# Products of old states with C placed behind weights' low parts, and logs of decays loaded one group at a time

## The chip, the cores and the metric

The kernel runs on one core of one Trainium2 chip, in one launch. The core has TensorE (PE in the profile; PEld is its loading of weights), VectorE (DVE), ScalarE (ACT) and GpSimd (POOL), which compute, and SyncE (SP), whose queue issues most of the transfers. The metric is the time of one execution on the device in microseconds, as the median over runs.

## The reference

One step of a hybrid decoder layer, for a prompt of 256 rows and 8 sequences that each decode one row. All of it is fp32; the model width is 2048. One input projection feeds windowed attention and a state-space mixer (32 heads of 64 in 4 groups, 128 states each); their outputs go through one output projection. Cross-attention and a convolutional feed-forward part follow, which the change doesn't touch.

```python
def ssd_scan(xs, dt, a, bm, cm, h0, chunk):
    ...
    la = jnp.cumsum(dt * a, axis=2)
    xdt = xs * dt[..., None]
    seg = la[:, :, :, None] - la[:, :, None, :]
    decay = jnp.exp(jnp.where(causal, seg, -jnp.inf))
    cb = jnp.einsum('bclgn,bcsgn->bclsg', cm, bm)
    y = jnp.einsum('bclsgh,bcsghp->bclghp', cb[..., None] * decay, xdt)
    decay_end = jnp.exp(la[:, :, -1:] - la)
    states = jnp.einsum('bcsgn,bcsghp->bcghpn', bm, xdt * decay_end[..., None])
    ...
    y = y + jnp.einsum('bclgn,bcghpn->bclghp', cm, h_prev) * jnp.exp(la)[..., None]

def ssd_mixer(z, xbc, dt_raw, conv_past, h0, ...):
    xbc, conv_new = causal_dwconv(xbc, conv_past, conv_w, conv_b)
    xbc = jax.nn.silu(xbc)
    ...
    y, h_last = ssd_scan(...)
    y = y + xs * d_skip
    y = y.reshape(b, t, D_SSD) * jax.nn.silu(z)
    y = rms_norm(y, norm_g)

def _layer(x, ...):
    proj = rms_norm(x, g_mix) @ w_in
    q, k, v, z, xbc, dt_raw = jnp.split(proj, IN_SPLITS, axis=-1)
    attn = swa_banded(q, k, v, sinks)        # or swa_step for the decode rows
    ssd, new_conv, new_h = ssd_mixer(z, xbc, dt_raw, ...)
    x = x + jnp.concatenate([attn, ssd], axis=-1) @ w_out
    x = x + cross_attend(x, ...)
    f, new_ffn = conv_ffn(x, ...)
    return x + f, ...
```

For a decode row the scan is one step: the output is C times the old state (128 states by 64 by 32 heads, for each sequence), scaled with the decay, plus what the row itself brings. These products of the old state with C are the 32 products of the title: a tile of 128 x 512 each, for one of 16 blocks of channels and four of the eight sequences.

## The kernel before

*Weights.* Every projection streams its weights from memory through weights() in parts of 128 x 1024 (512 KB, tile wraw, four buffers, issued on SP, L83). ScalarE rounds a part to its high half whi (L89), VectorE subtracts to get the low half wlo (L90), four buffers of each. mm3() multiplies in three passes, high by high, high by low, low by high (L104, L105, L106), so a part gives 24 matmuls with 264 columns (256 prompt rows and 8 decode rows). Parts 0 to 95 are w_in, 96 to 111 the first half of w_out, which meets the attention's output AT; from 112 on w_out meets the mixer's output Y.

*Order.* The code is not in the order in which it runs. A scheduler gives every instruction a place on its engine by the order of the code and by priority: weights() stands at high priority, and "with tc.issue_after(x)" puts what is inside behind x. Each engine then works through its list strictly in order, so an instruction that waits holds up all that is behind it. Tiles come from pools with few buffers: a load into a tile can't be issued before the last reader of that buffer is done.

*The mixer.* conv_group(g), g = 0 to 3, projects four blocks of channels of x by two calls of conv_pair (four weight parts each), does the causal convolution and SiLU for them (L769 on ScalarE, L771 and L773 on VectorE) and the decode rows by conv_sample. z_pair(i), i = 0 to 7, projects two blocks of the gate z and multiplies it into y. ssd_prompt(g) is the scan of the prompt for one group in two chunks. logs() loads what it needs: the cumulated logs of the decays, broadcast over partitions, into one tile called late (two loads of 512 KB, L824, and two of 128 KB, L828, on SP). Then ScalarE takes Relu of differences of logs (L846, 16 of 128 x 128 per group) and Exp (L847 twice, L889), VectorE multiplies with the products of C and B (L848), TensorE forms the output (L876) and the state of each chunk (L866), ScalarE copies the state of the first chunk to hp (L869), and the second chunk takes it up (L887, L894, L895).

*The decode rows' old states.* ssd_sample(g) loads C of the eight sequences, broadcast over partitions, into cb (512 KB, one buffer, on POOL's queue, L911); then, eight times, a piece of the old state into h (256 KB, three buffers, POOL's queue, L916), the product with cb (L917) and the sum over the states (L918), both on VectorE. The results ych are used only in gate_sample(), which finishes the decode rows of Y; it stands behind w_out's unit 4. It is called four times, behind conv_group(0), z_pair(1), z_pair(5) and w_out's unit 0. The scheduler is free to spread a call's instructions.

Of the kernel before, what the change touches and what calls it, by code (L numbers as in the profile page):

```python
# [7 lines left out]
F32 = mybir.dt.float32  # L8
F32R = mybir.dt.float32r
AF = mybir.ActivationFunctionType  # L10
ALU = mybir.AluOpType
# [37 lines left out]
def hybrid_decoder_step_kernel(ctx: ExitStack, tc: tile.TileContext, I, O):  # L49
    nc = tc.nc  # L50
# [25 lines left out]
    def weights(src, n=2048, into=None):  # L76

        out = []
        with tc.high_priority():
            for o in range(0, n, NPART):  # L80
                w = min(NPART, n - o)
                x = raw_part(w)
                marks["load"] = nc.sync.dma_start(out=x, in_=src[:, o:o + w])  # L83
                if into:
                    hi, lo = into
                else:
                    hi = wpool.tile([128, w], F32R, tag="whi", name="whi", bufs=WBUFS)
                    lo = wpool.tile([128, w], F32R, tag="wlo", name="wlo", bufs=WBUFS)
                S.copy(out=hi, in_=x)  # L89
                V.tensor_tensor(out=lo, in0=x, in1=hi.bitcast(F32), op=ALU.subtract)  # L90
                out.append((hi, lo))
        return out

# [5 lines left out]
                V.scalar_tensor_tensor(out=lo, in0=x, scalar=g, in1=hi.bitcast(F32), op0=ALU.mult, op1=ALU.subtract))  # L99

    marks = {}

    def mm3(out, wh, wl, xh, xl, start, stop):
        PE.matmul(out, wh, xh, start=start, stop=False)  # L104
# [94 lines left out]
    with tc.manual_schedule(engines={mybir.EngineType.SP, mybir.EngineType.PE, mybir.EngineType.Activation, mybir.EngineType.DVE}):  # L199
# [21 lines left out]
        for k in range(6):  # L221
            x_hi(k)
            lo = w_split(k, 1, k < 2)
# [74 lines left out]
    def total(acc, n, name, w=T, pool=None):  # L298
        p = psum("y")
        PE.matmul(p[:, :w], ones, acc, start=True, stop=True)  # L300
        r = pool.tile([128, w], F32, name=name) if pool else small.tile([128, w], F32, tag="r", name=name, bufs=2)
        rms(r, p[:, :w], n)
        return r
# [221 lines left out]
    def attn_prompt(j, rq, nrq, c, tag):  # L525
# [30 lines left out]
        for h in range(2):  # L556
            for kb in range(nb):
                tr(p[:, (h * nb + kb) * 128:(h * nb + kb) * 128 + 128], e[:, h, kb * 128:kb * 128 + 128])
        pt = mp.tile([128, 4, 128], F32, tag=tag, name="pt", bufs=2 if tag == "bc" else 1)
        S.copy(out=pt[:, 0:2 * nb, :], in_=p[:, 0:2 * nk].rearrange("p (a q) -> p a q", q=128))  # L560
        return pt

# [223 lines left out]
    def conv_pair(b0, dst):  # L786
        us = next_u()
        in_pair(lambda m, pm: V.tensor_tensor(out=us[:, m, 3:], in0=pm, in1=r0, op=ALU.mult))
        conv_side(b0, us, dst)
# [29 lines left out]
    def logs():  # L819

        g = len(lates)
        w = apool.tile([128, 8 * PITCH], F32, tag="B", name="late", bufs=4)
        for c in range(2):
            nc.sync.dma_start(out=w[:, 1024 * c:1024 * c + 1024].rearrange("p (h l) -> p h l", h=8),  # L824
                              in_=dram_la[c, 8 * g:8 * g + 8, :].partition_broadcast(128))
        ti = w[:, 2048:2560].rearrange("p (i l) -> p i l", i=4)
        for h in range(2):
            nc.sync.dma_start(out=ti[h * 64:h * 64 + 64], in_=lav[h][4 * g:4 * g + 4, :].partition_broadcast(64))  # L828
        lates.append(w)
# [76 lines left out]

    ych = mp.tile([128, KB, 8], F32, name="ych")

    def ssd_sample(g):
        cb = mp.tile([128, 8, 128], F32, tag="cb", name="cb", bufs=1)  # L910
        nc.gpsimd.dma_start(out=cb, in_=dram_bc[1][8 * g:8 * g + 8, :].partition_broadcast(128))  # L911
        for q in range(2):
            rows = slice(4 * q, 4 * q + 4)
            for i in range(4):
                h0 = mp.tile([128, 4, 128], F32, tag="h0", name="h0", bufs=3)
                nc.gpsimd.dma_start(out=h0, in_=I["h0"][4 * g + i][:, rows, :])  # L916
                V.tensor_tensor(out=h0, in0=h0, in1=cb[:, rows, :], op=ALU.mult)  # L917
                V.tensor_reduce(out=ych[:, 4 * g + i, rows], in_=h0, op=ALU.add, axis=AX.X)  # L918

    def conv_group(g):  # L920
        for i in (0, 2):
            conv_pair(4 * g + i, xs[g][:, i:i + 2, :TP])
        gs = slice(4 * g, 4 * g + 4)
        x = ysam[:, gs, :]
        conv_sample(4 * g, x)
        V.tensor_tensor(out=xds[:, gs, :], in0=x, in1=dsb[:, gs, 0:8], op=ALU.mult)
        V.tensor_tensor(out=x, in0=x, in1=pc("d_skip", 4 * g, 4).unsqueeze(2).broadcast_to([128, 4, 8]), op=ALU.mult)
# [43 lines left out]
        res.append(r)  # L971

    conv_group(0)
    ssd_sample(0)
    logs()
    logs()
    conv_group(1)
    ssd_prompt(0)
    conv_group(2)
    with tc.issue_after(marks["load"].ins):  # L980
# [3 lines left out]
    with tc.issue_after(marks["load"].ins):  # L984
        logs()
    nc.sync.dma_start(out=O["conv_new"], in_=cnew)
    z_pair(0)
    ssd_prompt(2)
    z_pair(1)
    ssd_sample(1)  # L990
    ssd_prompt(3)
    for i in range(2, 8):
        z_pair(i)
        if i == 5:
            ssd_sample(2)
        if i in (3, 5, 7):
            res_load()

# [8 lines left out]
    for i in range(8):  # L1007
        def ev(m, pm, i=i):
            k = 2 * i + m
            x = res[k // 4][:, k % 4, :]  # L1010
            V.tensor_tensor(out=x, in0=pm, in1=x, op=ALU.add)
        proj([w_out[i]], [AT], ev, tag="t" if i % 2 else "mm")
        if i == 0:
            ssd_sample(3)
        if i == 4:
            gate_sample()
    ry = total(accy, 4 * D, "ry")
    mix.close()
    cr = ExitStack()
# [623 lines left out]
```

## Time and profile before

| what | value |
|---|---|
| median of 3 runs | 1384.82 us (1384.39 to 1385.49) |
| the profiled execution | 1383.68 us, of which the span is 1381.9 |
| granted TensorE clock | 1.00 |
| PE busy | 1371.2 us, 99% of the span |
| DVE busy | 1042.7 us, 75% |
| ACT busy | 770.4 us, 56% |
| POOL busy | 92.2 us, 7% |
| moved by DMA | 298.31 MB, 216 GB/s in the mean |

The profile is one execution as the hardware profiler saw it. A row of the timeline gives the start in us from the span's begin, the length, the engine, the line, the operation and its tiles (out<-in), and in brackets how long the engine idled before it and what ended that. A view of waits gives, for an engine and a tile that waited, what it waited for, the us in total, the number of times and the longest. A view of a tile gives each operation on it with durations in ns (least, median, most) and, for transfers, the us from issue to landing. Windows give busy time per engine in a stretch. The mixer lies between about 150 and 415 us.

### The profile page before, as it was taken

The numbers are of one execution on the slowest core, as the hardware profiler recorded it, in microseconds if no ns is written. First come the engines' busy times: TensorE is split into PE (matmuls) and PEld (weight loads), VectorE is DVE, ScalarE is ACT, GpSimd is POOL, SyncE is SP. The second block draws the span as 40 slices with busy tenths as digits, with TensorE's granted clock in tenths as the row PEclk, the third lists the DMA queues.
The fourth block names the chain that finished last, engine by engine and source line by source line (L and its number), as shares of the span: only waits on it lengthen the run. The fifth ranks groups of instructions, "written<-read, shape, count | busy, mean of one in ns | idle before, by whom it ended". The sixth has DMA issues, their size and how long they took to land.

```text
span 1381.9 us, 28652 instructions
## 1 busy us (share of the span) xinstructions
PE 1371.2 (99%) x11412; PEld 1347.0 (97%) x11412; DVE 1042.7 (75%) x1797; ACT 770.4 (56%) x1255; POOL 92.2 (7%) x280
## 2 busy tenths in 40 slices
PE   9999989999999999999999999999999999999999
PEld 8999989999999999899999999999999999999998
DVE  8889889999967784579777765776577657765655
ACT  7667677644635555566565544554455445543532
POOL 0000010211000000002010000000000000000000
PEclk9999999999999999999999999999999999999999
DMA  7954588776575566866576766676667656655664
GB/s 301 328 159 152 162 285 273 234 233 202 176 274 175 189 226 213 312 235 198 185 259 215 259 214 184 214 258 214 185 213 244 198 184 200 198 183 184 194 186 139
DMA packets 88261, 298.31 MB, mean 216 GB/s; under 512 B 11840, under 2 KB 16960, under 8 KB 87616
## 3 DMA queue, kind: packets, MB, share of 16 engines
q1 hardware_dynamic: 82688, 277.61, 61.1%
q0 software_dynamic: 5440, 18.88, 4.1%
q8 instruction: 89, 1.46, 0.4%
q14 instruction: 44, 0.36, 0.1%
HBM read 280.77 MB, written 16.23 MB: 215 GB/s over the span
## 4 chain that ended last, share of the span: by engine, by line
PE 93%; DVE 3%; DMA 2%; ACT 1%; issue 1%; SPq 0%; ACTq 0%; DVEq 0%
PE mm L106 19%; PE mm L104 19%; PE mm L105 19%; PE t L106 9%; PE t L104 9%; PE t L105 9%; DVE wlo L90 1%; PE t L245 1%; DMA wraw<-in_w_in_dram 1%; PE t L283 1%; DMA h<-in_h_dram 1%; PE x L866 0%; DMA late<-dram_la 0%; DVE h L917 0%; DVE c L771 0%
## 5 line engine op out<-in xcount | busy, mean ns | idle before, releaser
L89 ACT CAST whi<-wraw 128x1024 fp32r<-128x1024 f32 x440 | 459.8, 1048 | 530.0 <-PE mm L105 264.1
L90 DVE TENSOR_TENSOR wlo<-wraw,whi 128x1024 fp32r<-128x1024 f32 x440 | 540.8, 1231 | 221.8 <-ACT whi L89 215.8
L106 PE MATMUL t<-x2h,wlo 128*128 128x264 f32 x704 | 198.6, 282 | 0.0
L104 PE MATMUL t<-x2h,whi 128*128 128x264 f32 x704 | 198.4, 282 | 0.0
L105 PE MATMUL t<-x2l,whi 128*128 128x264 f32 x704 | 198.4, 282 | 0.0
L105 PE MATMUL mm<-hl,whi 128*128 128x264 f32 x704 | 197.6, 282 | 0.0
L106 PE MATMUL mm<-hh,wlo 128*128 128x264 f32 x704 | 197.2, 282 | 0.0
L104 PE MATMUL mm<-hh,whi 128*128 128x264 f32 x704 | 195.7, 282 | 0.0
L104 PE MATMUL mm<-x2h,whi 128*128 128x264 f32 x672 | 189.4, 282 | 0.0
L105 PE MATMUL mm<-x2l,whi 128*128 128x264 f32 x672 | 189.4, 282 | 0.0
L106 PE MATMUL mm<-x2h,wlo 128*128 128x264 f32 x672 | 189.4, 282 | 0.0
L106 PE MATMUL mm<-xh,wlo 128*128 128x264 f32 x576 | 162.2, 287 | 3.8 <-DVE wlo L90 3.8
L104 PE MATMUL mm<-xh,whi 128*128 128x264 f32 x576 | 163.3, 285 | 0.0
L105 PE MATMUL mm<-xl,whi 128*128 128x264 f32 x576 | 162.6, 284 | 0.0
L106 PEld LDWEIGHTS t<-x2h,wlo 128*128 128x128 f32 x704 | 131.9, 187 | 0.0
L104 PEld LDWEIGHTS t<-x2h,whi 128*128 128x128 f32 x704 | 131.9, 187 | 0.0
L105 PEld LDWEIGHTS t<-x2l,whi 128*128 128x128 f32 x704 | 131.9, 187 | 0.0
L105 PEld LDWEIGHTS mm<-hl,whi 128*128 128x128 f32 x704 | 131.9, 187 | 0.0
L106 PEld LDWEIGHTS mm<-hh,wlo 128*128 128x128 f32 x704 | 131.7, 187 | 0.0
L104 PEld LDWEIGHTS mm<-hh,whi 128*128 128x128 f32 x704 | 130.8, 187 | 0.0
L104 PEld LDWEIGHTS mm<-x2h,whi 128*128 128x128 f32 x672 | 125.9, 187 | 0.0
L105 PEld LDWEIGHTS mm<-x2l,whi 128*128 128x128 f32 x672 | 125.9, 187 | 0.0
(522 smaller groups left out, 2927.3 us busy)
## 6 DMA issues: line engine op xcount, KB each, us to landing
wraw<-in_w_up_dram SPq DMA_DIRECT2D x176, 512.0 KB, 4.2
wraw<-in_w_in_dram SPq DMA_DIRECT2D x96, 512.0 KB, 4.5
wraw<-in_w_dn_dram SPq DMA_DIRECT2D x88, 512.0 KB, 4.3
wraw<-in_w_out_dram SPq DMA_DIRECT2D x48, 512.0 KB, 4.3
h<-in_h_dram POOLq DMA_DIRECT2D x32, 256.0 KB, 4.7
hn<-in_h_dram SPq DMA_DIRECT2D x16, 512.0 KB, 5.0
out_state_s_dram<-hn POOLq DMA_DIRECT2D x16, 512.0 KB, 3.8
late<-dram_la SPq DMA_DIRECT2D x8, 512.0 KB, 7.4
```

The lines of the kernel that those rows point to most:

```text
L89: S.copy(out=hi, in_=x)
L90: V.tensor_tensor(out=lo, in0=x, in1=hi.bitcast(F32), op=ALU.subtract)
L104: PE.matmul(out, wh, xh, start=start, stop=False)
L105: PE.matmul(out, wh, xl, start=False, stop=False)
L106: return PE.matmul(out, wl, xh, start=False, stop=stop)
L245: PE.matmul(first[c][:, :T], pre[k // 2][i][:, k % 2, c * 128:(c + 1) * 128], A[k // 8][x][:, k % 8, :], start=k + i + x == 0, stop=k == K ...
L283: return PE.transpose(out, in_, cst[0:k, C_ID:C_ID + k])
```

## The change

ssd_sample no longer does a whole group. An iterator over the 32 products is kept, and each call takes one or two of them; each is put by issue_after behind a given weight's low part: an argument d means the d-th last low part that weights() has made so far (lows, a list that weights() now fills). It is called after each conv_pair (one product, or two, behind the third last and the last low part, in conv_group; none after the first pair of group 0), after each z_pair, and after w_out's units 0 to 4 with two. cb is loaded in halves, four sequences at a time (256 KB, two buffers; the tile of pt, which shared its buffer, now has two as well unless its tag is hp). The call of logs() for group 1, which followed directly on that for group 0, now stands behind conv_group(1), behind the weight load that was last issued by then. gate_sample moves from w_out's unit 4 to unit 5. No arithmetic is added or dropped, but the tags' sizes and the scheduler's order change in other places, too. Lines behind L102 move by one, and those behind ssd_sample by more.

```diff
--- before.py
+++ after.py
@@ -87,7 +87,7 @@
                     hi = wpool.tile([128, w], F32R, tag="whi", name="whi", bufs=WBUFS)
                     lo = wpool.tile([128, w], F32R, tag="wlo", name="wlo", bufs=WBUFS)
                 S.copy(out=hi, in_=x)
-                V.tensor_tensor(out=lo, in0=x, in1=hi.bitcast(F32), op=ALU.subtract)
+                lows.append(V.tensor_tensor(out=lo, in0=x, in1=hi.bitcast(F32), op=ALU.subtract))
                 out.append((hi, lo))
         return out
 
@@ -99,6 +99,7 @@
                 V.scalar_tensor_tensor(out=lo, in0=x, scalar=g, in1=hi.bitcast(F32), op0=ALU.mult, op1=ALU.subtract))
 
     marks = {}
+    lows = []
 
     def mm3(out, wh, wl, xh, xl, start, stop):
         PE.matmul(out, wh, xh, start=start, stop=False)
@@ -556,7 +557,7 @@
         for h in range(2):
             for kb in range(nb):
                 tr(p[:, (h * nb + kb) * 128:(h * nb + kb) * 128 + 128], e[:, h, kb * 128:kb * 128 + 128])
-        pt = mp.tile([128, 4, 128], F32, tag=tag, name="pt", bufs=2 if tag == "bc" else 1)
+        pt = mp.tile([128, 4, 128], F32, tag=tag, name="pt", bufs=1 if tag == "hp" else 2)
         S.copy(out=pt[:, 0:2 * nb, :], in_=p[:, 0:2 * nk].rearrange("p (a q) -> p a q", q=128))
         return pt
 
@@ -906,20 +907,27 @@
 
     ych = mp.tile([128, KB, 8], F32, name="ych")
 
-    def ssd_sample(g):
-        cb = mp.tile([128, 8, 128], F32, tag="cb", name="cb", bufs=1)
-        nc.gpsimd.dma_start(out=cb, in_=dram_bc[1][8 * g:8 * g + 8, :].partition_broadcast(128))
-        for q in range(2):
+    todo = iter([(g, q, i) for g in range(4) for q in range(2) for i in range(4)])
+    held = {}
+
+    def ssd_sample(*behind):
+
+        for d in behind:
+            g, q, i = next(todo)
             rows = slice(4 * q, 4 * q + 4)
-            for i in range(4):
-                h0 = mp.tile([128, 4, 128], F32, tag="h0", name="h0", bufs=3)
-                nc.gpsimd.dma_start(out=h0, in_=I["h0"][4 * g + i][:, rows, :])
-                V.tensor_tensor(out=h0, in0=h0, in1=cb[:, rows, :], op=ALU.mult)
+            if i == 0:
+                held["cb"] = mp.tile([128, 4, 128], F32, tag="cb", name="cb", bufs=2)
+                nc.gpsimd.dma_start(out=held["cb"], in_=dram_bc[1][8 * g + 4 * q:8 * g + 4 * q + 4, :].partition_broadcast(128))
+            h0 = mp.tile([128, 4, 128], F32, tag="h0", name="h0", bufs=3)
+            nc.gpsimd.dma_start(out=h0, in_=I["h0"][4 * g + i][:, rows, :])
+            with tc.issue_after(lows[-d].ins):
+                V.tensor_tensor(out=h0, in0=h0, in1=held["cb"], op=ALU.mult)
                 V.tensor_reduce(out=ych[:, 4 * g + i, rows], in_=h0, op=ALU.add, axis=AX.X)
 
     def conv_group(g):
         for i in (0, 2):
             conv_pair(4 * g + i, xs[g][:, i:i + 2, :TP])
+            ssd_sample(*([3, 1] if i else [1] if g else []))
         gs = slice(4 * g, 4 * g + 4)
         x = ysam[:, gs, :]
         conv_sample(4 * g, x)
@@ -971,10 +979,10 @@
         res.append(r)
 
     conv_group(0)
-    ssd_sample(0)
-    logs()
     logs()
     conv_group(1)
+    with tc.issue_after(marks["load"].ins):
+        logs()
     ssd_prompt(0)
     conv_group(2)
     with tc.issue_after(marks["load"].ins):
@@ -984,15 +992,11 @@
     with tc.issue_after(marks["load"].ins):
         logs()
     nc.sync.dma_start(out=O["conv_new"], in_=cnew)
-    z_pair(0)
-    ssd_prompt(2)
-    z_pair(1)
-    ssd_sample(1)
-    ssd_prompt(3)
-    for i in range(2, 8):
+    for i in range(8):
         z_pair(i)
-        if i == 5:
-            ssd_sample(2)
+        ssd_sample(*([3, 1] if i in (1, 3, 5) else [1]))
+        if i < 2:
+            ssd_prompt(2 + i)
         if i in (3, 5, 7):
             res_load()
 
@@ -1010,10 +1014,11 @@
             x = res[k // 4][:, k % 4, :]
             V.tensor_tensor(out=x, in0=pm, in1=x, op=ALU.add)
         proj([w_out[i]], [AT], ev, tag="t" if i % 2 else "mm")
-        if i == 0:
-            ssd_sample(3)
-        if i == 4:
+        if i < 5:
+            ssd_sample(2, 1)
+        if i == 5:
             gate_sample()
+            assert next(todo, None) is None
     ry = total(accy, 4 * D, "ry")
     mix.close()
     cr = ExitStack()
```

What this does to the order, at three places. VectorE from before the low part of weight part 43 (wlo is a low part, h the old state, ych the sums; csm, sts and u belong to the convolution and the decode rows' attention); before:

```order
L917 TENSOR_TENSOR h_2452<-h_2452,cb 128x512
L764 COPY cnew<-u_655 128x22
L918 TENSOR_REDUCE ych<-h_2452 128x4
L778 TENSOR_TENSOR csm<-cnew,par 128x32
L779 TENSOR_TENSOR csm<-csm,cpc 128x32
L917 TENSOR_TENSOR h_2456<-h_2456,cb 128x512
L726 TENSOR_TENSOR sts<-sts 128x1
L917 TENSOR_TENSOR h_2460<-h_2460,cb 128x512
L918 TENSOR_REDUCE ych<-h_2456 128x4
L727 RECIPROCAL sts<-sts 128x1
L918 TENSOR_REDUCE ych<-h_2460 128x4
L90 TENSOR_TENSOR wlo<-wraw,whi 128x1024
```

The same engine after, from the low part of part 42 to that of part 43 and the product behind it:

```order
L90 TENSOR_TENSOR wlo<-wraw,whi 128x1024
L789 TENSOR_TENSOR u_655<-mm,r_423 128x264
L772 SCALAR_TENSOR_TENSOR c<-u_655,par,c 128x256
L720 TENSOR_REDUCE sts<-s 128x1
L772 SCALAR_TENSOR_TENSOR c<-u_655,par,c 128x256
L789 TENSOR_TENSOR u_655<-mm,r_423 128x264
L721 TENSOR_TENSOR sts<-sts,par 128x1
L772 SCALAR_TENSOR_TENSOR c<-u_655,par,c 128x256
L765 COPY cnew<-u_655 128x22
L722 TENSOR_SCALAR sts<-sts 128x1
L90 TENSOR_TENSOR wlo<-wraw,whi 128x1024
L924 TENSOR_TENSOR h_2589<-h_2589,cb 128x512
```

Three products and their sums stood right ahead of the low part of part 43; now none stands between the two low parts, and the next product follows the second.

ScalarE at the first 16 Relus (late, L846), with the casts of parts 41 and 42 just ahead of them; before:

```order
L89 CAST whi<-wraw 128x1024 x2
L846 ACTIVATE late<-late,la 128x128 x16
L722 ACTIVATE sts<-par,sts 128x1
L725 ACTIVATE own,sts<-s,sts 128x129
L89 CAST whi<-wraw 128x1024
L769 ACTIVATE c<-u_655,par 128x256 x2
L847 ACTIVATE late<-late 128x1024
L889 ACTIVATE late<-late 128x512
L781 ACTIVATE tsm<-csm 128x32
L847 ACTIVATE late<-late 128x1024
```

After, from the cast of part 42 on:

```order
L89 CAST whi<-wraw 128x1024
L770 ACTIVATE c<-u_655,par 128x256
L89 CAST whi<-wraw 128x1024
L770 ACTIVATE c<-u_655,par 128x256
L723 ACTIVATE sts<-par,sts 128x1
L726 ACTIVATE own,sts<-s,sts 128x129
L847 ACTIVATE late<-late,la 128x128 x5
L89 CAST whi<-wraw 128x1024
L847 ACTIVATE late<-late,la 128x128 x11
L782 ACTIVATE tsm<-csm 128x32
L890 ACTIVATE late<-late 128x512
L89 CAST whi<-wraw 128x1024
```

The Relus stood in one piece before the cast of part 43 (the row behind own); now that cast comes first, part 44's stands after five of them and part 45's after the rest.

SP's queue around the loads of the logs (dram_bc is the store of B and C that cb reads); before:

```order
L813 DMA dram_bc<-bcr 32x128
L83 DMA wraw<-in_w_in_dram 128x1024
L813 DMA dram_bc<-bcr 32x128
L83 DMA wraw<-in_w_in_dram 128x1024 x3
L824 DMA late<-dram_la 128x1024 x2
L828 DMA late<-dram_la 64x4x128 x2
L83 DMA wraw<-in_w_in_dram 128x1024 x5
L824 DMA late<-dram_la 128x1024 x2
L828 DMA late<-dram_la 64x4x128
```

After:

```order
L814 DMA dram_bc<-bcr 32x128
L83 DMA wraw<-in_w_in_dram 128x1024
L814 DMA dram_bc<-bcr 32x128
L83 DMA wraw<-in_w_in_dram 128x1024 x5
L825 DMA late<-dram_la 128x1024 x2
L829 DMA late<-dram_la 64x4x128 x2
L83 DMA wraw<-in_w_in_dram 128x1024 x3
L825 DMA late<-dram_la 128x1024 x2
L829 DMA late<-dram_la 64x4x128 x2
```

The first group's logs moved behind two more weight loads, and three instead of five stand between them and the second group's.

## Prediction

> **What bounds the kernel now.** I read the page's busy times first, then a table of windows, then TensorE's waits, and from each wait went back along the engine that ended it. Busy time by engine:
>
> ```profile
> PE 1371.2 (99%) x11412; PEld 1347.0 (97%) x11412; DVE 1042.7 (75%) x1797; ACT 770.4 (56%) x1255; POOL 92.2 (7%) x280
> ```
>
> TensorE is busy for 1371.2 of a span of 1381.9 us, so 10.7 us is all that any new order could save without shorter products. The change touches the mixer, roughly 150 to 415 us. The windows (length, then busy time of PE, PEld, DVE, ACT, POOL, then granted clock, DMA share and GB/s) say where the 10.7 us lie:
>
> ```profile
> core 0: us, PE busy (x) PEld busy (x) DVE busy (x) ACT busy (x) POOL busy (x), PEclk, DMA share, GB/s
> 20.00:180.00 160.00, 160.00 (x1394) 154.51 (x1393) 139.07 (x310) 113.76 (x229) 7.18 (x19) 1.00 0.64 208
> 180.00:192.00 12.00, 8.24 (x87) 7.65 (x89) 11.49 (x25) 8.50 (x13) 3.22 (x6) 1.00 0.65 208
> 192.00:212.00 20.00, 18.77 (x164) 18.29 (x156) 18.61 (x40) 15.80 (x32) 1.62 (x3) 1.00 0.85 283
> 212.00:220.00 8.00, 8.00 (x69) 8.00 (x68) 8.00 (x13) 5.10 (x10) 1.01 (x2) 1.00 0.88 289
> 220.00:280.00 60.00, 59.02 (x497) 55.83 (x497) 60.00 (x105) 39.82 (x73) 10.94 (x16) 1.00 0.82 263
> 280.00:1320.00 1040.00, 1039.90 (x8603) 1026.72 (x8603) 758.73 (x1238) 554.29 (x859) 67.98 (x232) 1.00 0.65 214
> ```
>
> In the mixer TensorE idles 3.76 us in 180 to 192, 1.23 in 192 to 212 and 0.98 in 220 to 280: 5.97 us together; the rest is at the kernel's two ends. These are three kinds of wait:
>
> ```profile
> PE mm L106 <- DVE wlo L90: 3.8, 2, 2.1
> PE t L104 <- ACT whi L89: 1.2, 1, 1.2
> PE x L866 <- ACT hp L869: 1.0, 1, 1.0
> ```
>
> and on TensorE's own timeline (start, length, what; in brackets the idle time and what ended it):
>
> ```profile
> 182.32 0.28 PE L105 MATMUL mm<-xl,whi 128*128 128x264 f32 x1
> 184.50 0.39 PE L106 MATMUL mm<-xh,wlo 128*128 128x264 f32 x1 [1.69 <-DVE wlo L90]
> 187.26 0.28 PE L105 MATMUL mm<-xl,whi 128*128 128x264 f32 x1
> 189.62 0.39 PE L106 MATMUL mm<-xh,wlo 128*128 128x264 f32 x1 [2.08 <-DVE wlo L90]
> 211.18 0.39 PE L104 MATMUL t<-xh,whi 128*128 128x264 f32 x1 [1.23 <-ACT whi L89]
> 277.06 0.70 PE L866 MATMUL x<-xw,Bn 128*128 128x512 f32 x1 [0.98 <-ACT hp L869]
> ```
>
> **Why the low parts are late.** VectorE ahead of the first two stalls:
>
> ```profile
> 172.69 1.21 DVE L90 TENSOR_TENSOR wlo<-wraw,whi 128x1024 fp32r<-128x1024 f32 x1
> 173.89 0.76 DVE L788 TENSOR_TENSOR u<-mm,r 128x264 f32<-128x264 f32 x2
> 178.43 0.69 DVE L917 TENSOR_TENSOR h<-h,cb 128x512 f32<-128x512 f32 x1 [3.78 <-DMA h<-in_h_dram]
> 181.38 0.69 DVE L917 TENSOR_TENSOR h<-h,cb 128x512 f32<-128x512 f32 x1 [0.51 <-DMA h<-in_h_dram]
> 183.24 1.22 DVE L90 TENSOR_TENSOR wlo<-wraw,whi 128x1024 fp32r<-128x1024 f32 x1
> 188.34 1.22 DVE L90 TENSOR_TENSOR wlo<-wraw,whi 128x1024 fp32r<-128x1024 f32 x1
> ```
>
> VectorE works in order, so it stood 3.78 us in front of a product whose old states had not landed. The low part behind that product ran at 183.24, after three products and their reduces; TensorE needed it at about 182.4. Call the weight part of this stall A, the part of the second stall B (low part at 188.34). In the chain of work that ended last, the load itself is a link:
>
> ```profile
> 173.00 8.35 DMA h<-in_h_dram
> ```
>
> ScalarE is the second reason. Its timeline:
>
> ```profile
> 170.56 1.05 ACT L89 CAST whi<-wraw 128x1024 fp32r<-128x1024 f32 x1 [2.59 <-issue]
> 174.81 4.80 ACT L846 ACTIVATE late<-late,la 128x128 f32<-128x128 f32 x16 [3.20 <-DMA late<-dram_la]
> 180.05 1.04 ACT L89 CAST whi<-wraw 128x1024 fp32r<-128x1024 f32 x1
> 180.99 1.09 ACT L769 ACTIVATE c<-u,par 128x256 f32<-128x256 f32 x2
> 181.98 1.04 ACT L847 ACTIVATE late<-late 128x1024 f32<-128x1024 f32 x1
> 184.51 2.93 ACT L89 CAST whi<-wraw 128x1024 fp32r<-128x1024 f32 x3
> ```
>
> It stood 3.20 us for the first logs, ran 16 Relus in 4.80 us, and cast part A only at 180.05 to 181.09. So even with no product in the way, A's low part could not have started before 181.1 and ended before 182.3. One reason alone doesn't carry the stall, and removing one alone would shorten it to nearly nothing but leave no reserve.
>
> **The change, part by part.** *Products spread out.* The 32 products and 32 reduces stay; no arithmetic is added. What they cost, and how their loads land:
>
> ```profile
> L916 POOL DMA_DIRECT2D h<-in_h_dram x32: 536/536/724, 150.4 to 310.8; - x32
> L917 DVE TENSOR_TENSOR h<-h,cb x32: 678/684/944, 167.7 to 320.7; 128x512 f32<-128x512 f32 x32
> L918 DVE TENSOR_REDUCE ych<-h x32: 667/678/689, 169.5 to 327.0; 128x4 f32<-128x512 f32 x32
> DMA to landing us min/median/max: 2.9/4.7/8.4
> ```
>
> That is 32 x (0.68 + 0.68) = 43.6 us of VectorE before and after. Before, the last reduce is at 327; now they run on to w_out's part 108, near 395. From 212 to 280 VectorE had no idle time at all (8.00 of 8.00, 60.00 of 60.00), so moving about a third of the 43.6 us behind 327 relieves the stretch in which its queue is full. Around A two products come first (with low part 39), then none until A's low part itself. Between the low part at 172.69 and A's now stand only two evacuations, three conv steps and small ones, about 3 us: A's low part is possible near 177, some 5 us before TensorE's 182.4. First stall gone: 1.69 us.
>
> *First group's logs two weight loads later.* On SP two more weight loads come first, and the buffer that they take comes free when the old keys are done on TensorE. My estimate of that is 173.5, by the place of that release in TensorE's order. Before:
>
> ```profile
> 168.29 0.80 SPq L824 DMA_DIRECT2D late<-dram_la  x2
> L846 ACT ACTIVATE late<-late,la x64: 385/388/404, 174.8 to 248.2; 128x128 f32<-128x128 f32 x64
> DMA to landing us min/median/max: 5.5/8.3/10.7
> ```
>
> The first Relu started 174.81 - 168.29 = 6.5 us after the issue. The bounds are 5.5 and 10.7, so the logs land between 179.0 and 184.2; I take 6.5, the same transfer in the same crowd, hence 180.0. In the new order ScalarE casts A before it looks at the logs, then does 5 Relus, casts B, does 11 Relus, casts the next. B's cast ends at 180.0 + 5 x 0.30 + 1.05 = 182.6, its low part near 184.0; TensorE wants it 24 products after A, 24 x 160.00/1394 = 2.75 us, with its small work about 185.4 (187.4 before, less the first stall). So the second stall goes too (2.08 us), with 1.4 us in hand; the part after B has 11 x 0.30 + 0.8 + 1.05 + 1.2 = 6.4 us to go from there and is wanted about 4.2 us later than B, margin 0 to 0.3 us.
>
> *What is late next: ScalarE.* From the logs' landing to the copy of group 0's carried state (hp, L869) I count in its new order 12 casts (2.93/3 each), 48 Relus (4.80/16), 5 Exps (1.0), three half Exps (0.6, half the length) and about 6 us of small work: 11.7 + 14.4 + 5 + 1.8 + 6 = 38.9, by overlapping starts 37.5 to 38.9. So hp is copied at 217.5 to 218.9 if the logs land at 180.0; by TensorE's order its second state product wants it at about 219.3 when nothing stalled before. The third stall (1.23 us, a cast behind Relus) is inside this stretch. Hence up to there TensorE's loss is about what the logs land after 180.3: nothing at 179.0, 3.9 us at 184.2. I take 0.6.
>
> *The fourth stall (0.98 us).* Group 1's second state product stood right behind group 1's own products, with hp not copied; now 23 rows separate them. The same pair of group 2 stands 27 rows apart, behind gate work of z_pair(0) on VectorE and ScalarE: bounds 0 and 2.0 us (the longest wait of this kind here, 2.1). I take 0.7.
>
> *C in halves.* 8 issues of 256 KB for 4 of 512 KB. Four more issues cost POOL 4 x 0.54 = 2.1 us; the windows show POOL busy for 10.94 of 60 us at most. Landing of the whole cb before (least, median, most):
>
> ```profile
> DMA to landing us min/median/max: 4.2/5.5/7.2
> ```
>
> A half lands between 2.9 (the fastest h) and 7.2 us. By POOL's order it is issued near 158.8, the first products want it at about 162.4: a wait of VectorE between 0 and 3.6 us, about 1 at the h loads' median of 4.7. Behind that stand conv steps and the next low parts, which there lie ready for some 5 us: the one before A ended at 172.69 + 1.21 = 173.9 and TensorE came to it one part before A, near 179.4. Nothing reaches the end.
>
> *gate_sample one unit later.* Before, its last instruction and TensorE's first use of it:
>
> ```profile
> 387.82 0.35 DVE L97 TENSOR_TENSOR yl<-ysam,yh 128x64 fp32r<-128x64 f32 x2
> 414.84 0.29 PE L105 MATMUL mm<-yl,whi 128*128 128x264 f32 x1
> ```
>
> 27 us of reserve. The last products now end near 396, the gate's chain behind them by my count of the order near 411.5: 3 us are left, no cost; without them each us later would be a us on TensorE.
>
> **Sum.** 1.69 + 2.08 + 1.23 + 0.98 = 5.98 us can go; new waits 0.6 + 0.7 and 0.2 for small slips on VectorE (low parts with 6 to 7 us of work between two of them) give 1.5. Net 4.5: the profiled execution, 1383.68 us (1381.9 of span and 1.8 around it), would become 1379.2. It lies 1.14 us under the median 1384.82, so the forecast against the median is 1380.3.
>
> **Rivals.** *The logs take the gain back.* If the first logs land near 183 to 184, B's low part and then hp are late by 3 to 4 us: net gain 1.0 to 2.5, 1382.3 to 1383.8. For it: the median landing of these queues' rows is above the 6.5 that I take, and nothing idle is left on ScalarE to catch up. Against: before, with the same loads ahead, 6.5.
>
> *Nothing changes:* if the scheduler's pins only swap which instruction waits, 1384.8. Against: in the new order no product stands in front of A at all.
>
> *Slower: pinned products block VectorE.* A product now stands at a fixed low part; if its load is late, all later low parts wait. A load may be issued when the product three before it is reduced, so it has two to three parts' time, 6.6 to 9.9 us at 3.3 us a part (2.75 and a fifth for the mixer's small products, my estimate), against 2.9 to 8.4 of landing. It costs something once landing passes 6.6 plus the 2 to 5 us for which low parts lie ready, 8.6 us; at 8.4 that is just not reached. For a slower kernel (over 2.8 us more, after 5.98 saved) it would have to add 8.8 us: five waits of 1.8 us, landing at 10.4, giving 1388. [...]
>
> **How the numbers follow.** A change under 0.2% (2.8 us) is about what a measurement can't tell from none; faster means under 1382.0, slower over 1387.6. Forecast, net 3 to 6 us: 0.66, all faster. Logs take it back: 0.18, of which 0.04 faster and 0.14 the same. Nothing: 0.07. Blocked VectorE: 0.09, of which 0.08 slower. That makes 0.70 faster, 0.22 same, 0.08 slower. The low end is 1384.82 - 5.98 and 0.6 for the spread of runs, 1378.2; the high end takes in the logs' rival and nearly no change, 1384.3.
>
> **What would show it.** TensorE's waits for low parts near 182 and 187 gone, VectorE without a wait for h between 174 and 182; first Relu at about 180; busy time in 180 to 192 near 12.0; a wait for hp of under 1 us near 219; the product rows spread to 395. I am wrong if the first Relu starts after 182, if VectorE waits for h more than three times, or if TensorE waits for yh or yl at 414.

## The result, and the profile after

The changed kernel takes 1381.08 us in the median of 8 runs (1378.73 to 1382.51), the kernel before 1385.13 in the same session: a ratio of 0.9969 with an interval of 0.9958 to 0.998, 4.05 us or 0.3% faster. Eleven more runs of the same kernel (e4 below) give 1381.46 and a ratio of 0.998 (0.9972 to 0.9989). The forecast was 1380.3, in 1378.2 to 1384.3.

The profiled execution of the changed kernel took 1382.16 us (span 1380.4), one of its slower ones: 1.5 us less than the profiled one of before. Its windows over the mixer, columns as in the prediction:

```profile
180.00:192.00 12.00, 12.00 (x124) 11.66 (x123) 8.29 (x16) 12.00 (x26) 1.08 (x2) 1.00 0.66 215
192.00:212.00 20.00, 18.51 (x140) 18.09 (x139) 16.98 (x36) 16.08 (x34) 0.54 (x1) 0.91 0.78 243
...
220.00:280.00 60.00, 58.57 (x503) 56.45 (x500) 56.53 (x98) 37.19 (x63) 10.49 (x13) 1.00 0.69 215
```

From 180 to 192 the 3.76 us of idle time are gone to nothing. From 192 to 212 there are 1.49 us (before 1.23), and the granted clock is 0.91, where it was 1.00: 16 matmuls there start 0.22 us apart instead of 0.12, which is 1.6 us more. From 220 to 280 there are 1.43 us (before 0.98). Idle time fell from 5.97 to 2.92, and the slower clock took back 1.6: about 1.4 us net, close to the 1.5 us by which the spans differ. TensorE's waits now:

```profile
PE x L867 <- ACT hp L870: 1.4, 1, 1.4
...
PE mm L105 <- DVE u L789: 1.1, 1, 1.1
PE mm L105 <- ACT whi L89: 0.4, 1, 0.4
```

The two waits for low parts aren't there. VectorE shows why: part A's low part runs at 175.28, ahead of the product, where it ran at 183.24 behind three products; part B's at 181.44 instead of 188.34.

```profile
175.28 1.22 DVE L90 TENSOR_TENSOR wlo<-wraw,whi 128x1024 fp32r<-128x1024 f32 x1
176.41 0.69 DVE L924 TENSOR_TENSOR h<-h,cb 128x512 f32<-128x512 f32 x1
...
181.44 1.22 DVE L90 TENSOR_TENSOR wlo<-wraw,whi 128x1024 fp32r<-128x1024 f32 x1 [1.96 <-ACT whi L89]
```

New are two waits close together near 201 us, and the clock behind them (TensorE's timeline):

```profile
200.91 0.39 PE L105 MATMUL mm<-xh,whi 128*128 128x264 f32 x1 [0.40 <-ACT whi L89]
...
202.51 0.39 PE L105 MATMUL mm<-xh,whi 128*128 128x264 f32 x1 [1.09 <-DVE u L789]
...
203.03 0.42 PE L105 MATMUL mm<-xh,whi 128*128 128x264 f32 x1
203.25 0.42 PE L106 MATMUL mm<-xl,whi 128*128 128x264 f32 x1
...
206.33 0.29 PE L107 MATMUL mm<-xh,wlo 128*128 128x264 f32 x1
206.45 0.28 PE L105 MATMUL mm<-xh,whi 128*128 128x264 f32 x1
```

From 203.03 on the matmuls start every 0.22 us and last 0.42, up to about 206.2; then again every 0.12 us. ScalarE says what the first of the two waits came from:

```profile
178.89 1.57 ACT L847 ACTIVATE late<-late,la 128x128 f32<-128x128 f32 x5 [2.85 <-DMA late<-dram_la]
...
194.66 2.45 ACT L847 ACTIVATE late<-late,la 128x128 f32<-128x128 f32 x8 [2.03 <-DMA late<-dram_la]
197.47 2.45 ACT L847 ACTIVATE late<-late,la 128x128 f32<-128x128 f32 x8 [0.36 <-DMA late<-dram_la]
199.82 1.03 ACT L89 CAST whi<-wraw 128x1024 fp32r<-128x1024 f32 x1
```

The first logs' Relus start at 178.89, the second logs' at 194.66 and 197.47 after waits, and the cast of a weight part stands behind them until 199.82. The chain of work that ended last goes through the same transfer:

```profile
172.12 1.06 PE s L716 x32
173.20 5.67 DMA late<-dram_la
...
188.93 8.52 DMA late<-dram_la
...
200.89 1.23 DVE wlo L90
202.12 0.68 DVE u L789 x2
```

VectorE waits in order for that cast, makes the low part at 200.89, and only then evacuates two accumulators (u, L789), for which TensorE waits the second time.

### The profile page after: what moved, and what is told of

It reads as the page before. It is cut to its first block, busy times and chain, and to the rows that moved or that the text cites. A ratio compares the mean times of both kernels' runs of the same rounds, so it can differ in the third digit from the quotient of the medians.

```text
span 1380.4 us, 28658 instructions
## 1 busy us (share of the span) xinstructions
PE 1372.4 (99%) x11412; PEld 1348.3 (98%) x11412; DVE 1044.4 (76%) x1797; ACT 770.5 (56%) x1255; POOL 92.1 (7%) x284
## 4 chain that ended last, share of the span: by engine, by line
PE 93%; DMA 2%; ACT 2%; DVE 1%; issue 1%; SPq 0%; ACTq 0%
PE mm L106 20%; PE mm L105 20%; PE mm L107 20%; PE t L107 9%; PE t L105 9%; PE t L106 9%; DMA late<-dram_la 2%; ACT late L847 1%; PE t L246 1%; PE t L284 1%; DVE wlo L90 1%; PE mm L246 0%; PE s L246 0%; ACT whi L89 0%; PE x L867 0%
## 5 line engine op out<-in xcount | busy, mean ns | idle before, releaser
L105 PE MATMUL mm<-x2h,whi 128*128 128x264 f32 x672 | 189.4, 282 | 0.0
L106 PE MATMUL mm<-x2l,whi 128*128 128x264 f32 x672 | 189.4, 282 | 0.0
L107 PE MATMUL mm<-x2h,wlo 128*128 128x264 f32 x672 | 189.4, 282 | 0.0
```

The lines of the kernel that those rows point to most:

```text
L106: PE.matmul(out, wh, xl, start=False, stop=False)
L107: return PE.matmul(out, wl, xh, start=False, stop=stop)
```

## The experiments

All times are medians; each kernel was timed beside the kernel before on the same chip (1384.77 us for e1 to e4, 1385.15 for e5 to e8, 1385.23 for e9 to e11, 1385.05 for e12).

**The edit of logs() alone changes nothing.** The changed kernel with both calls of logs() put back behind conv_group(0), and the kernel before with the second call moved, have on all five engines the same order of instructions as without that edit (names' numbers and line numbers apart). There is no run of it: the effect comes from the other edits, the places of the products and C above all. The first logs' loads do move by two weight loads, but through those.

**e1: only the first eight products.** The kernel before, with a first_sample that places the eight products of group 0 as the changed kernel does; C stays whole, the 24 others as before.

```diff
-    ssd_sample(0)
...
             conv_pair(4 * g + i, xs[g][:, i:i + 2, :TP])
+            first_sample(*([3, 1] if i else [1] if g else []))
```

> The kernel before, with only the first group's eight products placed behind low parts as in the changed kernel; the 24 later products, C in one piece and gate_sample stay as before. In the order of instructions the first logs' Relus stand ahead of part A's cast again, as before. Theory 1 (the gain comes from the products that stood ahead of the low parts of A and B): TensorE's wait for A falls from 1.7 us to under 0.5, B's from 2.1 to under 1.5; 2 to 4 us faster than before, about 1381.1 to 1383.1. Rival (the gain comes from the 24 later products, which relieve VectorE from 212 to 327): under 1 us faster, 1384 to 1385. Rival 2 (ScalarE's Relus ahead of the cast are enough to make A late): waits for A and B of over 1 us each remain, 1383 to 1385.

1378.36 us, ratio 0.996 (0.9947 to 0.9972): 6.4 us faster than before and faster than the changed kernel. ScalarE's Relus stand ahead of A's cast as before, A's low part follows that cast at once, and TensorE idles 0.10 us (timelines of ScalarE and VectorE, then the window):

```profile
175.85 4.49 ACT L847 ACTIVATE late<-late,la 128x128 f32<-128x128 f32 x15
...
181.30 1.23 DVE L90 TENSOR_TENSOR wlo<-wraw,whi 128x1024 fp32r<-128x1024 f32 x1 [3.59 <-ACT whi L89]
```

```profile
180.00:192.00 12.00, 11.90 (x122) 11.49 (x122) 10.70 (x22) 11.88 (x27) 0.56 (x2) 1.00 0.73 233
```

Theory 1 holds in what waits, and the gain is larger than its 2 to 4 us; what else may be in it is said under e7. Both rivals fall.

**e2: C in one piece.** The changed kernel without the halves; the tile of pt is back at one buffer, as before.

```diff
-            if i == 0:
-                held["cb"] = mp.tile([128, 4, 128], F32, tag="cb", name="cb", bufs=2)
+            if i == 0 and q == 0:
+                held["cb"] = mp.tile([128, 8, 128], F32, tag="cb", name="cb", bufs=1)
```

> The changed kernel with C loaded in one piece of 512 KB (one buffer, as before); all 32 products placed as in the changed kernel. In its order the loads of the first logs stand where they stood before (two weight loads earlier than in the changed kernel), the second ones two loads earlier. Theory 1 (what is lost in the changed kernel near 200 us comes from the second logs' late landing): the wait of a cast near 200 and the halved clock behind it go, waits near 182 stay under 0.5 us; 1378 to 1381, at least as fast as the changed kernel. Rival (the halves of C are needed, since a product waits for the whole C and a low part behind it): a wait of VectorE for cb over 4 us and waits of TensorE for low parts; 1382 to 1385.

1378.47 us, ratio 0.9955 (0.9943 to 0.9967), 2.8 us under the changed kernel (1381.27, the mean of its two medians above). Its only wait of TensorE inside the mixer:

```profile
PE mm L107 <- DVE wlo L90: 0.4, 1, 0.4
```

So the changed kernel gave that back through the halves of C; how, e5 shows.

**e3: no products at all.** ssd_sample does nothing and ych is zero, so the kernel leaves the old states' share out of its result.

```diff
+    V.memset(ych, 0.0)
     def ssd_sample(*behind):
-        for d in behind:
...
+        pass
```

> The changed kernel without the old states' loads, the 32 products and their sums, and without the loads of C for them (ych is set to zero, so the decode rows lack the old states' share). Theory 1 (the products as placed now cost TensorE nothing; what is left is ScalarE's logs and copies): within 1.5 us of the changed kernel either way, 1379 to 1382. Rival (the products still delay low parts, by VectorE's time): 3 us or more faster than the changed kernel, 1377 to 1378, which is TensorE without any wait.

1382.08 us in 12 runs, ratio 0.9983 (0.9973 to 0.9992). Taking 43.6 us off VectorE doesn't make the kernel faster than the changed one. The scheduler gave it another order with waits of its own (hp 2.7 us in two, 1.9 and 1.3 us elsewhere), so it bounds nothing more exactly; as a test of what the products cost it is inconclusive.

**e4: the changed kernel again,** without an edit.

> The changed kernel again, unchanged, for its clock beside its time on this chip. Theory 1 (the spread of its times comes from the clock that halves behind the two short waits near 200 us in some executions): times in two groups some 2 to 3 us apart, the slower ones with a mean clock of 0.998 or 0.999 and PE clock under 1 in 192 to 212. Rival (the spread is that of transfers): no relation of time and clock.

1381.46 us, 1379.64 to 1385.0. No two groups: with a mean clock of 1.000 the runs lie from 1379.64 to 1383.07, with 0.998 or 0.999 from 1381.46 to 1385.0. Its profiled execution has the clock at 1.00 everywhere and other waits than the first one (hp 3.0 us in two; 13.6 us of waits of ScalarE for logs, where the first had 11.8). So the clock is a part of the spread and the landing of the logs another; theory 1 was half right.

**e5: why the halves cost.** The halves are back; the first two products stand behind the decode attention's copies into zz.

```diff
-            with tc.issue_after(lows[-d].ins):
+            with tc.issue_after((marks["zz"] if (g, q) == (0, 0) and i < 2 else lows[-d]).ins):
```

> The changed kernel (C in halves) with one difference: the first two products stand behind the decode attention's copies into zz instead of behind low parts. In its order zz, the release of the old keys' buffer and with it the first logs' loads stand where they stood in the kernel before. Theory 1 (what the changed kernel loses against e2 comes from the two first products standing ahead of zz, which makes the logs 5 us later; the halves themselves cost nothing): logs' first load issued near 168, first Relu near 175, TensorE's waits in the mixer under 1 us together, 1377.5 to 1379.5. Rival (C's halves cost by their four more transfers): 1380.5 to 1382, as the changed kernel.

1378.91 us, ratio 0.9957 (0.9945 to 0.997): as e2, though TensorE waits 1.5 us for hp, where under 1 us had been expected. The halves themselves cost nothing that shows in the time. In the changed kernel the scheduler had put the first two products ahead of zz (the tile with the decode rows' queries, and later their weights, which TensorE multiplies with the old keys and values). The old keys kcT and values vc lie in buffers that the logs take over. In the changed kernel VectorE's copies to zz and TensorE's products with the keys (L716) and the values (L739) ran at

```profile
169.88 0.58 DVE L710 COPY zz<-qs_sq 64x32 f32<-64x32 f32 x4
...
172.05 1.09 PE L716 MATMUL s<-kcT,zz 128*32 128x129 f32 x32
...
184.78 1.08 PE L739 MATMUL s<-vc,zz 128*32 128x128 f32 x32
```

and in e2 at

```profile
165.85 0.59 DVE L710 COPY zz<-qs_sq 64x32 f32<-64x32 f32 x4
...
167.66 1.09 PE L716 MATMUL s<-kcT,zz 128*32 128x129 f32 x32
...
180.04 1.08 PE L739 MATMUL s<-vc,zz 128*32 128x128 f32 x32
```

The copies are 4.0 us apart, the products 4.4 and 4.7. The end of those with the keys frees the buffer of the first logs, the end of those with the values that of the second.

**e6: the first logs late, alone.** e2 with the first logs' loads behind two more weight loads.

```diff
     conv_group(0)
-    logs()
...
             conv_pair(4 * g + i, xs[g][:, i:i + 2, :TP])
+            if (g, i) == (1, 2):
+                with tc.issue_after(loads[-2].ins):
+                    logs()
```

> e2 (C in one piece, all products placed) with the first logs' loads held behind two more weight loads, as in the changed kernel; the products stand as in e2. Theory 1 (later logs alone cost what the changed kernel loses against e2): first Relu 4 to 5 us later than in e2, casts behind it late, waits of TensorE of 2 to 5 us between 180 and 260; 1380 to 1382.5. Rival (the logs' time doesn't matter; the difference lies in the products' places): 1377.5 to 1379.5.

1378.32 us, ratio 0.9957 (0.9944 to 0.9969): as e2, although its first block of Relus starts at 180.22 instead of 175. Theory 1 falls here: first logs that are as late as in the changed kernel cost nothing. The second logs' loads were issued at 182.59 in e6, 182.26 in e2, 183.10 in e5 and 187.92 in the changed kernel, which leads to theory 2, tested by e9.

**e7: the first eight in a block again.** e2 with the first group's products in one unplaced block and the 24 others placed.

```diff
     conv_group(0)
+    ssd_block()
...
-            ssd_sample(*([3, 1] if i else [1] if g else []))
+            if g:
+                ssd_sample(*([3, 1] if i else [1]))
```

> e2 with the first group's eight products in one block, unplaced, as in the kernel before; the 24 later ones placed as in e2. Theory 1 (the first eight make the gain): waits for the low parts of A and B return with 3 to 4 us together, 1382.5 to 1384.5. Rival (the 24 later ones make it, by relieving VectorE from 212 to 327): 1378 to 1380.5.

1383.11 us, ratio 0.999 (0.9981 to 0.9999). The old waits are back (TensorE's waits; then, by itself, a window of 2 us behind the longer one):

```profile
PE mm L107 <- DVE wlo L90: 3.3, 2, 2.7
```

```profile
186.00:188.00 2.00, 2.00 (x12) 2.00 (x11) 2.00 (x6) 0.70 (x1) 0.00 (x0) 0.50 0.67 240
```

So placing the 24 later products is worth about 2 us here, and nothing between e1 and e2; the first eight make the gain.

They may make it in two ways, which e1 and e7 don't separate. In the kernel before and in e7 the block of products also stands among the decode attention's steps on VectorE. TensorE's products with the old values run at 191.25 in the kernel before and at 180.00 in e1, and with the block the second logs are later still than in the changed kernel (SP in before, e7, the changed kernel and e2):

```profile
192.39 0.80 SPq L824 DMA_DIRECT2D late<-dram_la  x2
...
193.29 1.05 SPq L825 DMA_DIRECT2D late<-dram_la  x2
...
187.92 1.43 SPq L825 DMA_DIRECT2D late<-dram_la  x2
...
182.26 1.45 SPq L825 DMA_DIRECT2D late<-dram_la  x2
```

So "late" is meant against e2: the change brought the second logs forward by 4.5 us, and e2 and e1 (182.97) by about 10. No run has the block and early second logs; e9 has the second logs late without the block, and gives up 2.8 of e2's 6.3 us (each against the kernel before on its own chip).

**e8: Relus behind later casts.** The changed kernel; the second group's Relus behind the cast of part 50, the fourth's behind one of a later part.

```diff
-            with tc.issue_after(marks["attn"].ins):
+            with tc.issue_after((highs[{1: 50, 3: 64}[g]] if g in {1: 50, 3: 64} else marks["attn"]).ins):
                 for j in range(8):
```

> The changed kernel with the Relus of the second group put behind the cast of weight part 50 and those of the fourth behind a later cast, so that no cast stands behind a wait for these logs; loads and products stay where they are. Theory 1 (the casts behind waiting Relus near 194 and 243 us make the changed kernel's remaining waits and their spread): waits near 200 and for hp near 255 fall to under 1 us together, 1378 to 1380. Rival (ScalarE is simply full; moving Relus only moves the wait to hp): within 0.7 us of the changed kernel.

1383.8 us, ratio 0.9992 (0.9983 to 1.0001): slower than the changed kernel, which neither theory 1 nor the rival had. The edit had missed one instruction: the half Exp of the second logs now stood first and waited 5.98 us for its own small transfer, with the cast behind it; TensorE waited 2.2 us there and 2.1 for hp. The queue was the same, with another instruction at its head.

**e9: the second logs late, alone.** e2 with the second logs' loads behind two more weight loads.

```diff
     conv_group(1)
-    with tc.issue_after(marks["load"].ins):
-        logs()
...
             conv_pair(4 * g + i, xs[g][:, i:i + 2, :TP])
+            if (g, i) == (2, 0):
+                with tc.issue_after(loads[49].ins):
+                    logs()
```

> e2 (C in one piece) with the second logs' loads held behind two more weight loads, near 188 us instead of 182 as in the changed kernel; the first logs and the products stay. Theory 2 (in the changed kernel the decode attention ends later, its buffer comes free later, and it is the second logs, not the first, that land too late for the casts queued behind them on ScalarE): ScalarE waits for them near 192 to 196, TensorE waits 1 to 3 us near 200, some executions with a halved clock behind that; 1380 to 1382.5. Rival (it is the places of the first products, or the later decode attention itself): 1377.5 to 1379.3, as e2.

1381.75 us, ratio 0.9973 (0.9963 to 0.9984): about the changed kernel's loss, made in e2 by moving the second logs alone. They are issued 1.3 us later than in the changed kernel. The issue on SP and ScalarE's wait for it:

```profile
189.25 1.50 SPq L827 DMA_DIRECT2D late<-dram_la  x2
...
195.79 2.16 ACT L849 ACTIVATE late<-late,la 128x128 f32<-128x128 f32 x7 [3.33 <-DMA late<-dram_la]
```

and TensorE's waits:

```profile
PE x L869 <- ACT hp L872: 2.9, 2, 1.8
```

Theory 2 holds in the time. In the profiled execution TensorE's waits between 200 and 206 are 0.6 us for low parts and 0.5 for a copy, and 2.9 us come later, for hp, where theory 2 had 1 to 3 us near 200: here most of ScalarE's delay reached TensorE through hp.

**e10 and e11: casts ahead of all work on these logs.** As e8, with the half Exp behind the casts too; e10 for the second and fourth logs, e11 for the second.

```diff
-        S.activation(out=ti, in_=ti, func=AF.Exp)
+        with tc.issue_after((highs[{1: 50, 3: 64}[g]] if g in {1: 50, 3: 64} else marks["attn"]).ins):
+            S.activation(out=ti, in_=ti, func=AF.Exp)
```

> The changed kernel with all that ScalarE does on the second and fourth logs as soon as they land (Relus and the half Exp, which e8 had left in place) behind later casts, so that no cast up to part 50 stands behind a wait for the second logs. Theory 2: the wait near 200 us goes (it was 1.5 us, and 2.2 in e8), the clock stays at 1.00 there; 1378 to 1380.5, what is left being hp near 250. Rival (later logs make the group's own work late in any order): a wait of 1.5 us or more for hp or for low parts instead, 1381 to 1384.

> As e10 for the second logs alone; those of the fourth group stay as in the changed kernel. Theory 2: wait near 200 us gone, and a wait for hp near 250 of 1 to 3 us as in the changed kernel; 1379 to 1381.5. Rival (only where the fourth logs stand matters): as the changed kernel, 1381 to 1382.

1380.29 us, ratio 0.9965 (0.9952 to 0.9978), and 1380.96, ratio 0.9967 (0.9954 to 0.9979): about 1.0 and 0.3 us under the changed kernel, within its spread. In e11 the wait near 200 is gone and one of 1.6 us for hp is left, as expected. In e10 hp's went, but the wait near 200 stayed (1.7 us), for another reason (ScalarE, then SP):

```profile
201.70 1.05 ACT L89 CAST whi<-wraw 128x1024 fp32r<-128x1024 f32 x1 [6.61 <-DMA wraw<-in_w_in_dram]
...
189.36 1.14 SPq L826 DMA_DIRECT2D late<-dram_la  x2
...
192.29 12.07 SPq L83 DMA_DIRECT2D wraw<-in_w_in_dram  x5
```

The cast waited 6.61 us for its weights, which were issued at 192.29, right behind the four loads of the second logs, and landed 9.4 us later. The logs in turn were issued at 189.36, although TensorE's last use of their buffer ended at 186.9: on SP a weight load stood ahead of them.

**e12: the second logs on another queue.** e10, with the four loads of the second logs on POOL's queue.

```diff
+        eng = nc.gpsimd if g == 1 else nc.sync
         for c in range(2):
-            nc.sync.dma_start(out=w[:, 1024 * c:1024 * c + 1024].rearrange("p (h l) -> p h l", h=8),
+            eng.dma_start(out=w[:, 1024 * c:1024 * c + 1024].rearrange("p (h l) -> p h l", h=8),
...
-            nc.sync.dma_start(out=ti[h * 64:h * 64 + 64], in_=lav[h][4 * g:4 * g + 4, :].partition_broadcast(64))
+            eng.dma_start(out=ti[h * 64:h * 64 + 64], in_=lav[h][4 * g:4 * g + 4, :].partition_broadcast(64))
```

> e10 with one difference: the second logs' four loads are issued on POOL's queue instead of SP's, so that no weight load stands behind their wait for a free buffer. Theory 2, second half (in e10 the cast of part 50 waited 6.6 us for a weight load that had stood behind the second logs on SP): that weight load is issued before 189 instead of 192, the wait of 1.7 us near 200 goes, the clock stays at 1.00; 1378 to 1379.5. Rival (the transfers of that stretch are simply slow, whichever queue they are on; or the old states' loads behind the logs on POOL become late): a wait of over 1 us near 200 remains, or VectorE waits for h; 1380 to 1382.

1377.72 us, ratio 0.995 (0.9937 to 0.9964), the lowest median of all, though e1, e2 and e6 lie within 0.8 us of it. POOL issues the logs at 186.32, as soon as TensorE has freed their buffer, and TensorE's only wait in the mixer is one of 1.0 us for a copy (timelines of SP and POOL, then TensorE's waits):

```profile
176.49 25.52 SPq L83 DMA_DIRECT2D wraw<-in_w_in_dram  x8
...
186.32 1.06 POOL L827 DMA_DIRECT2D late<-dram_la  x2 [7.26 <-PE s L740]
```

```profile
PE t L285 <- ACT oss L742: 1.0, 1, 1.0
```

The time is 0.3 us under the expected range, and the expectation had one thing wrong: the weight load of part 50 was to be issued before 189 us and is issued at 191.8, since it waits for its own buffer; what moved is the logs, 3 us earlier, and part 50 is cast at 199.14 instead of 201.70 (0.5 us of it by issue, the rest by a shorter landing). So the second logs' lateness seems to cost in two ways: casts stood on ScalarE behind work that waited for them, and a weight load that went out right behind them landed later (9.4 us after its issue in e10, 7.3 in e12). The second way is read from one execution each of e10 and e12. How the loss divides between the two is not settled: e10 took away the first alone, and its gain is within the spread.

## Why the prediction was right, point by point

*The two stalls at A and B (1.69 and 2.08 us).* Right in mechanism: gone in the changed kernel, in e1 and in e2, back in e7. That one of the two reasons alone leaves next to nothing is what e1 shows, with the Relus in place and 0.10 us of idle time. Mis-sized: the price of these stalls was taken as their length. The mean granted clock of the 65 runs of the kernel before beside the experiments is 0.9986, which is 0.0014 x 1383 = 1.9 us of work a run, and 1.0000 in 20 runs of e2, e5, e6 and e12. The profiled execution of before, on which the sum rests, had 1.00 throughout, so this term was absent from it.

*The first logs.* The estimate was right: issue at 173.5 forecast, 173.20 measured, first Relu 180.0 against 178.89 and, in e4, 179.84. The step behind it was wrong: "up to there TensorE's loss is about what the logs land after 180.3". By that rule the profiled execution would have lost nothing up to hp; it lost 1.49 us of idle time and 1.6 by the clock, where the sum had 0.6. In e6 the first logs came as late and next to nothing was lost up to hp (0.14 us), as the rule has it; e9 made the second logs late and lost 2.8 us, for which the rule has no term. What I took for one queue of ScalarE, set off by the first logs, was a queue set off again by the second, which I hadn't followed in the order.

*The third and fourth stall.* The third (1.23 us) was to go into that 0.6: in its place stand 0.40 + 1.09 us and the halved clock. The fourth was bounded by 0 and 2.0 with 0.7 taken; the same wait for hp measured 1.4 us, and 2.1 in e4, which had another 0.9 for group 0's hp. Together the new losses are 2.92 us of idle time and 1.6 of clock in the profiled execution, against 1.5 in the sum. Two terms missed, then: the clock in the price of the old stalls, which raises the gain, and what the second logs still cost, which lowers it. That they nearly cancel, so that a sum of 4.5 came near 4.05, is luck.

*C in halves.* "Nothing reaches the end" failed. The wait of VectorE for the first half was as forecast, and was harmless; but the earlier half let the scheduler put two products ahead of zz, and that made both logs later than in e2 (e5). The order shown ahead of the prediction had the displaced loads of the logs; their cause was not looked for. VectorE's waits for operands of the products in the changed kernel:

```profile
DVE h L924 <- DMA cb<-dram_bc: 1.3, 1, 1.3
...
DVE h L924 <- DMA h<-in_h_dram: 0.6, 1, 0.6
```

and, from the view of the old states' tile (least, median, most):

```profile
DMA to landing us min/median/max: 3.0/4.5/8.5
```

*The slower rival.* These rows also speak against it: one product waited for old states, 0.6 us, and landings stayed within 8.5 us although the products are pinned.

*VectorE's relief from 212 to 327.* Idle time of VectorE in 220 to 280 went from none to 3.47 us, but it bought little: e1 is as fast without it, and e7, which has it alone, gains 2.0 us at most.

*gate_sample.* Forecast near 411.5 with 3 us in hand; its low parts run at 409.23 and TensorE takes them up at 413.03. No wait.

```profile
409.23 0.35 DVE L97 TENSOR_TENSOR yl<-ysam,yh 128x64 fp32r<-128x64 f32 x2
...
413.03 0.29 PE L106 MATMUL mm<-yl,whi 128*128 128x264 f32 x1
```

*The rival "the logs take the gain back".* Given 0.18, it named the right tile and the wrong load: against e2, 2.8 us were taken back, by the second logs.

## What to carry to other kernels

A change of a few small instructions can act through a chain that none of them is in: two products ahead of a copy, the copy ahead of a matmul, the matmul ahead of a buffer, the buffer ahead of a transfer, and behind that transfer everything in two queues. So after an edit look first at which transfers moved in their queue, and ask for each what released it, and what stands behind it while it waits; undoing one edit at a time (e2, e5) found 6.3 us here where the whole change has 3.3 to 4.05. A profiled execution is one execution: compare its granted clock with that of the other runs before a stall is priced at its length.

## What the runs showed of the hardware

Stalls of TensorE cost more than their length in some executions. In the changed kernel's profile two waits of 0.40 and 1.09 us within 2.5 us were followed by about 3.3 us (202.9 to 206.2) at a clock of 0.50, which is 1.6 us of work; in e7 a wait of 2.74 us by 3.4 us (186.0 to 189.4) at 0.50, while in the profiled execution of before two waits of 1.69 and 2.08 us were followed by none. The kernels with under 2 us of waits in the mixer (e1, e2, e5, e6 and e12) had a mean clock of 1.000 in 24 of 25 runs, and the one of e1 with 0.999, its profiled one, has 1.00 in every window up to 1320 us and 0.97 in the last, from there to the end; those with the two old stalls had 0.9986 (before, 65 runs) and 0.9986 (e7, 11 runs). Both slow stretches are about as long, 3.3 and 3.4 us, behind waits of 1.49 us together and of 2.74. What decides whether one follows on a stall is not shown by any run here.
